# Score heads without a gate: one 128-row stationary [q hi; q lo] for both score matmuls

## The chip, the cores and the metric

The kernel runs on one core of one Trainium2 chip. The metric is the device time of one execution in microseconds; lower is better. TensorE (PE) does the matmuls, VectorE (DVE), ScalarE (ACT) and GpSimd (POOL) the elementwise work, and SyncE (SP) issues every DMA.

## The reference

Two transformer blocks run one after the other on 512 tokens of width 1024. The first has a pooling branch, twelve heads of dilated attention and a gated MLP. The second has four differential heads (two score maps each), six forgetting heads, six chunk heads, a convolution in its MLP and a final gated embedding. Every attention score has the same core, here from the second block:

```python
def probs(qb, k):
    s = jnp.einsum('bqhd,bkhd->bhqk', qb, k).astype(jnp.float32) * scale + bias
    s = jnp.where(allowed, s, NEG_INF)
    return jax.nn.softmax(s, axis=-1)
```

A head is 64 wide. The forgetting heads alone add a per-token gate (a cumulative sum of log f) to the score.

## The kernel before

All matmuls work on pairs of 32-bit tiles: a value x is kept as hi (x rounded to the matmul's type) and lo = x - hi, and a product is the sum of hi·hi, hi·lo and lo·hi. ACT makes hi and DVE makes lo (`split`, L179 and L180, or L182 and L183 with a scale).

The order of the attention stages is written out by hand in two strings, `ORDER1` (first block, `mix1`) and `ORDER2` (second block, `mix2`): P projects a pair of heads to q and k, T turns that pair into score operands, V makes values, S computes the four score blocks of one head, W transposes the probabilities and weighs the values. A planner then sets the order of instructions on each engine from this program, with its own estimate of durations; each engine executes its list in order.

T is `to_heads`. It transposes q and k of a pair (two heads of 64, L310) into two PSUM tiles, qT and kT, of 128 rows by 512 tokens. These come from a pool of three banks, from which projections and values take their banks too. It splits each of them over all 128 rows (two ACT and two DVE instructions), and then copies rows by DMA into operands: for each head, a tile k1 with k hi in the head's own 64 rows and k lo in the other 64, and a tile q1 with q hi in both halves. That is four copies of 64x512 a head, 128 KB each, eight a pair (`copy`, L379).

S calls `probs` for each block of 128 queries. Its two matmuls add into one bank: L255, of 128 stationary rows, gives hi·hi + hi·lo; L256 multiplies q lo by k hi. For heads without a gate L256 has the head's own 64 rows of the tiles, for the six forgetting heads 68 rows (64 plus four of the gate), copied to rows 0 to 67 of tiles of their own. The columns are 128, 256, 384 or 512. Then DVE adds the table (L259), ACT takes the exponential (L114), DVE the reciprocal (L263) and POOL scales (L267). W's transposes are L277, its matmuls L285 and L286. L189 to L191 and L352 to L354 are the three matmuls of a dense product.

There are 16 pairs, six in the first block and ten in the second. Three of them are the forgetting pairs; 13 have no gate.

Of the kernel before, what the change touches and what calls it, by code (L numbers as in the profile page):

```python
# [9 lines left out]
F32 = mybir.dt.float32  # L10
F32R = mybir.dt.float32r
AF = mybir.ActivationFunctionType
ALU = mybir.AluOpType
AX = mybir.AxisListType

P = 128
# [46 lines left out]
class Builder:  # L63
# [240 lines left out]
    def to_heads(self, z, gq, gk, extra=None):  # L304
        nc = self.nc
        qT, kT = self.psum(), self.psum()
        for d, o in ((qT, 0), (kT, P)):
            ins = {}
            for t in (3, 2, 1, 0):
                ins[t] = nc.tensor.transpose(d[:, t * P:t * P + P],  # L310
                                             z[t // 2][:, (t % 2) * 256 + o:(t % 2) * 256 + o + P], self.ident)
                if t < 3:
                    self.after(ins[t].ins, ins[3].ins.name)
        qh, ql = self.split(qT, gq, tag="k")
        ops = []
        kh, kl = self.split(kT, 1.0 if gk is None else gk, tag="k")
        ks = [self.slot("k", F32R) for _ in range(2)]
        for e in range(2):
            a, b = slice(64 * e, 64 * e + 64), slice(64 - 64 * e, P - 64 * e)
            k1, q1 = ks[e], self.slot("k", F32R)  # L320
            self.copy(k1[b], kl[a])
            self.copy(k1[a], kh[a])
            self.copy(q1[a], qh[a])
            self.copy(q1[b], qh[a])
            if extra is None:
                ops.append((q1, k1, ql[a], k1[a]))
                continue
            fr, i = extra
            q2, k2 = self.slot("k", F32R), self.slot("k", F32R)
            self.copy(q2[0:64], ql[a])  # L330
            self.copy(k2[0:64], k1[a])
            self.copy(q2[64:68], fr[i][4 * e:4 * e + 4])
            self.copy(k2[64:68], fr[i][32 + 4 * e:36 + 4 * e])
            ops.append((q1, k1, q2[0:68], k2[0:68]))
        return ops
# [673 lines left out]
```

## Time and profile before

| | us |
|---|---|
| median of three timed runs | 1374.2 (1372.47 to 1374.73) |
| span of the profiled execution, first to last instruction | 1373.6 |
| PE busy in it | 1345.1 (98%) |
| DVE busy | 842.4 (61%) |
| ACT busy | 657.9 (48%) |
| attention of the first block | about 45 to 192 |
| attention of the second block | about 690 to 912 |

The profiled execution's span is 0.6 us under the median; no other time is given for it. A matmul's recorded duration contains time in which its neighbours run too, so the pace of PE is read from the distance between the starts of successive matmuls, not from durations. The busy share says little about the attention stages, where the stretches with many small matmuls must be read one by one.

### The profile page before, as it was taken

The page shows a single profiled execution, that of the slowest core. Times are in us where ns is not written, and L with a number is a line of the kernel's source. Part 1 is how long each engine was busy: PE and PEld are TensorE (multiplying, and loading weights), DVE is VectorE, ACT ScalarE, POOL GpSimd, SP SyncE. Part 2 cuts the span into 40 slices and gives each one's busy share as a digit, 9 for nine tenths or more (in the row PEclk, how much of TensorE's full clock was granted, in tenths as well). Part 3 has the DMA queues.
Part 4 walks back from the last instruction along what each step waited for, and adds up shares of the span by engine and source line. Part 5 has one row for each costly group of instructions (what it writes and reads, how often), then busy time and mean ns, then how long its engine had stood idle before and what let it go on. Part 6 is the DMA issues. An engine that isn't in the chain of part 4 may idle for free.

```text
span 1373.6 us, 20168 instructions
## 1 busy us (share of the span) xinstructions
PE 1345.1 (98%) x7450; PEld 1147.6 (84%) x7450; DVE 842.4 (61%) x1713; ACT 657.9 (48%) x1285; POOL 206.6 (15%) x240
## 2 busy tenths in 40 slices
PE   9999999899999999997999999999999999999998
PEld 9888878788888888886988899778888888888887
DVE  6666785864444433239667877666777777743345
ACT  6465645543333332236465767664554444522242
POOL 1223222400000000016222334441000000000010
PEclk9999999999999999998999999999999999999999
DMA  5532433132233322326264345433432223332222
GB/s 199 142 95 67 117 103 123 50 120 92 92 95 103 95 92 92 95 84 229 93 155 125 104 121 147 110 100 115 140 99 92 92 92 98 101 101 92 92 92 77
DMA packets 52962, 148.52 MB, mean 108 GB/s; under 512 B 7072, under 2 KB 7968, under 8 KB 52864
## 3 DMA queue, kind: packets, MB, share of 16 engines
q1 hardware_dynamic: 52864, 147.24, 35.0%
q8 instruction: 58, 0.95, 0.3%
q14 instruction: 40, 0.33, 0.1%
HBM read 122.38 MB, written 6.29 MB: 94 GB/s over the span
## 4 chain that ended last, share of the span: by engine, by line
PE 89%; DVE 6%; DMA 2%; issue 1%; ACT 1%; POOL 1%; SPq 0%; DVEq 0%; POOLq 0%; ACTq 0%
PE p L190 20%; PE p L189 20%; PE p L191 20%; PE p L352 6%; PE p L353 6%; PE p L354 6%; PE p L256 3%; PE p L277 2%; PE p L255 2%; DVE sv L559 1%; PE p L286 1%; DVE sh L183 1%; PE p L285 1%; DVE wl L170 1%; PE p L310 1%
## 5 line engine op out<-in xcount | busy, mean ns | idle before, releaser
L166 ACT ACTIVATE wh<-wr 128x512 fp32r<-128x512 f32 x417 | 260.5, 631 | 409.9 <-PE p L190 350.4
L170 DVE TENSOR_TENSOR wl<-wr,wh 128x512 fp32r<-128x512 f32 x398 | 285.9, 724 | 224.7 <-ACT wh L166 218.2
L190 PE MATMUL p<-sh,wh 128*128 128x512 f32 (+1 forms) x858 | 323.1, 378 | 8.6 <-DVE sh L183 8.6
L191 PE MATMUL p<-sh,wl 128*128 128x512 f32 (+1 forms) x858 | 322.5, 377 | 0.0
L189 PE MATMUL p<-sh,wh 128*128 128x512 f32 (+1 forms) x858 | 318.6, 376 | 0.0
L352 PE MATMUL p<-wh,sh 128*128 128x256 f32 (+1 forms) x736 | 212.4, 290 | 3.3 <-ACT sz L446 2.4
L354 PE MATMUL p<-wh,sh 128*128 128x256 f32 (+1 forms) x736 | 210.7, 288 | 4.6 <-DVE sh L183 4.6
L353 PE MATMUL p<-wl,sh 128*128 128x256 f32 (+1 forms) x736 | 211.8, 289 | 0.2 <-DVE wl L170 0.2
L190 PEld LDWEIGHTS p<-sh,wh 128*128 128x128 f32 x858 | 162.7, 190 | 40.7 <-DVE sh L183 10.2
L191 PEld LDWEIGHTS p<-sh,wl 128*128 128x128 f32 x858 | 162.9, 190 | 31.5 <-issue 0.7
L189 PEld LDWEIGHTS p<-sh,wh 128*128 128x128 f32 x858 | 161.3, 190 | 32.0 <-issue 1.0
L352 PEld LDWEIGHTS p<-wh,sh 128*128 128x128 f32 x736 | 141.4, 192 | 8.3 <-issue 2.9
L354 PEld LDWEIGHTS p<-wh,sh 128*128 128x128 f32 x736 | 140.8, 192 | 8.0 <-DVE sh L183 5.7
L353 PEld LDWEIGHTS p<-wl,sh 128*128 128x128 f32 x736 | 141.3, 193 | 3.6 <-issue 1.9
L267 POOL TENSOR_SCALAR sp<-sp,m 128x128 f32<-128x128 f32 (+1 forms) x112 | 69.7, 626 | 181.4 <-DVE m L263 164.2
L114 ACT ACTIVATE sp<-sp,m 128x128 f32<-128x128 f32 (+3 forms) x128 | 71.6, 561 | 45.6 <-DVE m L259 42.1
L170 POOL TENSOR_TENSOR wl<-wr,wh 128x512 fp32r<-128x512 f32 (+1 forms) x19 | 25.6, 1345 | 447.9 <-ACT wh L166 447.7
L191 PE MATMUL p<-so,wl 128*128 128x512 f32 (+1 forms) x246 | 88.4, 360 | 0.2 <-DVE wl L170 0.2
L190 PE MATMUL p<-so,wh 128*128 128x512 f32 (+1 forms) x246 | 88.4, 360 | 0.0
L259 DVE CUSTOM_DVE_ANT_0 sp<-p,sm 128x128 f32<-128x128 f32 (+3 forms) x128 | 61.1, 486 | 44.3 <-PE p L256 32.4
L189 PE MATMUL p<-so,wh 128*128 128x512 f32 (+1 forms) x246 | 87.9, 361 | 0.2 <-ACT so L179 0.2
L190 PE MATMUL p<-sk,wh 128*128 128x512 f32 (+1 forms) x184 | 67.1, 365 | 0.0
(201 smaller groups left out, 2075.0 us busy)
## 6 DMA issues: line engine op xcount, KB each, us to landing
wr<-in_w_gu SPq DMA_DIRECT2D x88, 512.0 KB
wr<-in_w_down SPq DMA_DIRECT2D x44, 512.0 KB
sk<-sk SPq DMA_DIRECT2D x140, 128.0 KB
wr<-in_w_qk SPq DMA_DIRECT2D x31, 512.0 KB
wr<-in_w_out SPq DMA_DIRECT2D x12, 512.0 KB
sv<-in_x SPq DMA_DIRECT2D x16, 256.0 KB
wr<-in_w_ple_gate SPq DMA_DIRECT2D x8, 512.0 KB
wr<-in_w_v SPq DMA_DIRECT2D x6, 512.0 KB
```

Source lines behind the costliest of these rows:

```text
L114: i = self.nc.scalar.activation(out, in_, func, **k)
L166: nc.scalar.activation(hi[:, :w], c, AF.Copy)
L170: eng.tensor_tensor(lo[:, :w], c, hi[:, :w].bitcast(F32), ALU.subtract)
L189: mm(out, lhsT=ahi, rhs=bhi, start=start, stop=False)
L190: mm(out, lhsT=ahi, rhs=blo, start=False, stop=False)
L191: mm(out, lhsT=alo, rhs=bhi, start=False, stop=stop)
L256: nc.tensor.matmul(ps[:, :n], lhsT=q2[:, c], rhs=k2[:, :n], start=False, stop=True)
L259: nc.vector.tensor_tensor_reduce(p[:, :n], ps[:, :n], tab[:, (3 - qb) * P:S], 1.0, 3e38, ALU.add, ALU.min, accum_out=m[:, 0:1])
L267: self.nc.gpsimd.tensor_scalar(p[:, :n], p[:, :n], m[:, 2:3], 1.0, ALU.mult, ALU.mult)
L352: mm(d, lhsT=h[k][0][:, a], rhs=hi[:, c], start=k == 0 and (o == 0 or not first), stop=False)
L353: mm(d, lhsT=h[k][0][:, a], rhs=lo[:, c], start=False, stop=False)
L354: mm(d, lhsT=h[k][1][:, a], rhs=hi[:, c], start=False, stop=k == 7 and (o > 0 or not first))
```

## The change

For pairs without a gate `to_heads` now makes the operands by itself, head by head. With a the head's own 64 rows and b the other 64: ACT writes q hi to rows a of a tile q, and DVE writes q lo to rows b of the same tile, reading rows a. ACT writes k hi to rows a of a tile kh, DVE k lo to rows a of a tile kl. Two DMA copies then double kh and kl into rows b. Both score matmuls have q as their stationary operand, with 128 rows; the first has kh as its moving operand, the second kl. Together they give hi·hi + lo·hi + hi·lo + lo·lo. The forgetting pairs keep the old way, in a function of their own.

```diff
+        if extra is not None:
+            return self.heads_with_rows(qT, kT, gq, gk, *extra)
+        ops = []
+        gk = 1.0 if gk is None else gk
+        per = lambda g, r: g if isinstance(g, float) else g[r]
+        for e in range(2):
+            a, b = slice(64 * e, 64 * e + 64), slice(64 - 64 * e, P - 64 * e)
+            q, kh, kl = (self.slot("k", F32R) for _ in range(3))
+            nc.scalar.activation(q[a], qT[a], AF.Copy, scale=per(gq, a))
+            nc.vector.scalar_tensor_tensor(q[b], qT[a], per(gq, a), q[a].bitcast(F32), ALU.mult, ALU.subtract)
+            nc.scalar.activation(kh[a], kT[a], AF.Copy, scale=per(gk, a))
+            nc.vector.scalar_tensor_tensor(kl[a], kT[a], per(gk, a), kh[a].bitcast(F32), ALU.mult, ALU.subtract)
+            self.copy(kh[b], kh[a])
+            self.copy(kl[b], kl[a])
+            ops.append((q, kh, q, kl))
+        return ops
+
+    def heads_with_rows(self, qT, kT, gq, gk, fr, i):
         qh, ql = self.split(qT, gq, tag="k")
+        kh, kl = self.split(kT, gk, tag="k")
         ops = []
-        kh, kl = self.split(kT, 1.0 if gk is None else gk, tag="k")
...
-            if extra is None:
-                ops.append((q1, k1, ql[a], k1[a]))
-                continue
-            fr, i = extra
```

In the changed file the four new instructions are L322 and L324 (ACT), L323 and L325 (DVE); later lines are numbered 14 higher (the copy L393, projections L366 to L368). The tiles sk are score operands, p is PSUM, wh and wl are weights, sz a projected pair.

On ACT, at the first pair of the first block, before (a bracket names the engines waited for):

```order
L446 ACTIVATE sz_593<-p_544 128x512 [waits DVE_49,PE_49,Pool_49]
L182 ACTIVATE sk_611<-p_601 128x512 [waits PE_49]
L182 ACTIVATE sk_615<-p_602 128x512 [waits PE_49]
L166 ACTIVATE wh_1003<-wr_1001 128x512 [waits DMAHW0_49,Activation_49]
L374 ACTIVATE sv_631<-p_635,rc_204 128x4x64 [waits PE_49]
```

And now:

```order
L460 ACTIVATE sz_593<-p_544 128x512 [waits DVE_49,PE_49,Pool_49]
L322 ACTIVATE sk_611<-p_601 64x512 [waits PE_49]
L324 ACTIVATE sk_612<-p_602 64x512 [waits PE_49]
L322 ACTIVATE sk_620<-p_601 64x512 [waits DVE_49]
L324 ACTIVATE sk_621<-p_602 64x512 [waits DVE_49]
L166 ACTIVATE wh_999<-wr_997 128x512 [waits DMAHW0_49,Activation_49]
L388 ACTIVATE sv_629<-p_633,rc_204 128x4x64 [waits PE_49]
```

Two instructions became four, and those of the second head wait for DVE, which reads the same PSUM tile for the first head.

On DVE at the same place, before:

```order
L170 TENSOR_TENSOR wl_986<-wr_979,wh_985 128x512
L183 SCALAR_TENSOR_TENSOR sk_612<-p_601,sk_611 128x512
L183 SCALAR_TENSOR_TENSOR sk_616<-p_602,sk_615 128x512
L453 TENSOR_TENSOR sz_593<-sz_593,sm_212 128x512
L454 TENSOR_TENSOR sz_593<-sz_593,sz_594 128x8x32
```

And now:

```order
L170 TENSOR_TENSOR wl_982<-wr_975,wh_981 128x512
L323 SCALAR_TENSOR_TENSOR sk_611<-p_601,sk_611 64x512
L325 SCALAR_TENSOR_TENSOR sk_613<-p_602,sk_612 64x512
L467 TENSOR_TENSOR sz_593<-sz_593,sm_212 128x512
L323 SCALAR_TENSOR_TENSOR sk_620<-p_601,sk_620 64x512
L468 TENSOR_TENSOR sz_593<-sz_593,sz_594 128x8x32
L469 TENSOR_TENSOR sz_593<-sz_593,sz_594 128x8x32
L325 SCALAR_TENSOR_TENSOR sk_622<-p_602,sk_621 64x512
```

The second head's two instructions stand in between the rotation of the next pair (L467 to L469).

On PE, at the first scores of the second block (rows 3802 to 3808 of PE's list; a matmul reads its moving and then its stationary tile), before:

```order
L352 MATMUL p_7134<-wh_7077,sh_5750 128x256
L353 MATMUL p_7134<-wl_7078,sh_5750 128x256
L255 MATMUL p_6841<-sk_6827,sk_6829 128x128
L256 MATMUL p_6841<-sk_6827,sk_6820 128x128
L255 MATMUL p_6849<-sk_6797,sk_6799 128x128
L256 MATMUL p_6849<-sk_6797,sk_6790 128x128
L354 MATMUL p_7134<-wh_7077,sh_5751 128x256
```

And now (rows 3754 to 3760):

```order
L366 MATMUL p_7032<-wh_7061,sh_5738 128x256
L367 MATMUL p_7032<-wl_7062,sh_5738 128x256
L255 MATMUL p_6825<-sk_6806,sk_6805 128x128
L255 MATMUL p_6833<-sk_6778,sk_6777 128x128
L256 MATMUL p_6833<-sk_6779,sk_6777 128x128
L368 MATMUL p_7032<-wh_7061,sh_5739 128x256
L366 MATMUL p_7118<-wh_7035,sh_5724 128x256
```

The transposes of both pairs stand where they stood (from row 3697), so the first score has come 48 rows nearer to them; and the first matmul with k lo, L256 of the second pair, no longer follows its L255 at once.

## Rows read from the trace of the kernel before

**Rows 1.** The page: the chain that ended last, by engine.

```profile
PE 89%; DVE 6%; DMA 2%; issue 1%; ACT 1%; POOL 1%; SPq 0%; DVEq 0%; POOLq 0%; ACTq 0%
```

**Rows 2.** Timeline of PE: start us, duration us, line, tiles, rows*columns, moving operand; 64-row scores.

```profile
58.32 0.32 PE L256 MATMUL p<-sk,sk 64*128 64x128 f32 x1
58.58 0.38 PE L255 MATMUL p<-sk,sk 128*128 128x256 f32 x1
...
60.77 0.50 PE L255 MATMUL p<-sk,sk 128*128 128x512 f32 x1
61.20 0.50 PE L256 MATMUL p<-sk,sk 64*128 64x512 f32 x1
61.63 0.38 PE L352 MATMUL p<-wh,sh 128*128 128x256 f32 x1
...
69.29 0.40 PE L255 MATMUL p<-sk,sk 128*128 128x512 f32 x1
69.62 0.50 PE L256 MATMUL p<-sk,sk 64*128 64x512 f32 x1
...
908.37 0.50 PE L256 MATMUL p<-sk,sk 64*128 64x512 f32 x1
```

**Rows 3.** The same view at scores of forgetting heads, with 68 rows.

```profile
821.09 0.40 PE L255 MATMUL p<-sk,sk 128*128 128x512 f32 x1
821.33 0.40 PE L256 MATMUL p<-sk,sk 68*128 68x512 f32 x1
821.57 0.28 PE L352 MATMUL p<-wh,sh 128*128 128x256 f32 x1
...
825.22 0.28 PE L256 MATMUL p<-sk,sk 68*128 68x128 f32 x1
825.33 0.33 PE L353 MATMUL p<-wl,sh 128*128 128x256 f32 x1
```

**Rows 4.** Groups by form, count | busy us, mean ns | idle before: weight loads of L256.

```profile
L256 PEld LDWEIGHTS p<-sk,sk 64*128 64x128 f32 x104 | 19.3, 186 | 18.0 <-issue 13.1
L256 PEld LDWEIGHTS p<-sk,sk 68*128 68x128 f32 x24 | 4.5, 189 | 0.0
```

**Rows 5.** The same view: splits of T, and 64-row instructions of W.

```profile
L183 DVE SCALAR_TENSOR_TENSOR sk<-p,gq,sk 128x512 fp32r<-128x512 f32 x20 | 14.7, 742 | 1.6 <-ACT sk L182 1.4
L290 DVE TENSOR_TENSOR so<-p,st 64x512 f32<-64x512 f32 x28 | 19.2, 687 | 14.4 <-ACT st L289 13.9
L289 ACT ACTIVATE st<-p 64x512 f32<-64x512 f32 x28 | 16.6, 592 | 22.7 <-PE p L286 22.4
```

**Rows 6.** Timeline of SP's queue: the eight copies of one pair.

```profile
145.73 5.55 SPq L379 DMA_DIRECT2D sk<-sk  x8
```

**Rows 7.** Windows: stretch, length, busy us of PE, PEld, DVE, ACT, POOL, granted clock.

```profile
160.00:190.00 30.00, 30.00 (x147) 22.77 (x146) 26.27 (x74) 18.22 (x48) 10.30 (x13) 1.00 0.48 140
784.00:849.00 65.00, 65.00 (x525) 63.51 (x525) 48.60 (x146) 45.71 (x111) 27.29 (x31) 1.00 0.51 138
```

**Rows 8.** End of the first attention: timeline of DVE, then the chain (start, length, step).

```profile
178.13 0.68 DVE L290 TENSOR_TENSOR so<-p,st 64x512 f32<-64x512 f32 x1 [0.33 <-ACT st L289]
...
191.31 1.03 DVE wl L170
...
192.38 0.50 PE p L191
```

**Rows 9.** The chain in the second attention, 870 to 878 us.

```profile
870.44 0.60 PE p L277 x4
...
876.14 1.27 POOL sm L705
...
877.79 0.48 PE p L255
```

**Rows 10.** Timelines before the second block's first scores: DVE, then PE.

```profile
698.85 1.41 DVE L183 SCALAR_TENSOR_TENSOR sk<-p,gq,sk 128x512 fp32r<-128x512 f32 x2 [0.90 <-ACT sk L182]
...
706.29 0.22 PE L255 MATMUL p<-sk,sk 128*128 128x128 f32 x1
```

## The prediction

> **What bounds the kernel now.** I read the page's chain that ended last first: 89% of it is PE and 1% is issue [rows 1]. So time comes off this kernel only where PE's own list gets shorter, or where PE waits less. Next I read the timeline of PE around the scores, by the distance between successive starts. With 512 columns, a score of a forgetting head takes 0.24 us for L255 and 0.24 for L256 [rows 3]. The same block without a gate takes 0.43 and 0.43 at 60.77 us, or 0.33 and 0.43 at 69.29 [rows 2]. The columns are the same, the first matmul is the same; the difference is the second one, with 64 rows in place of 68. PE stands still on both sides of it: L256 starts 0.09 or 0.19 late, and what follows starts 0.19 late. The groups by form tell it too: the 104 weight loads of 64 rows have 18.0 us of idle time before them, 13.1 of it with no releaser that the profile shows, the 24 of 68 rows none [rows 4]. That it is no wait for data follows from the regularity, and from the missing releaser.
>
> **The gain: L256 with 128 rows.** The part after: for 384 and 256 columns I find the same 0.19 as for 512; for 128 columns it is 0.26 from start to start against 0.11 with 68 rows [rows 2, 3], 0.15 more. That makes 78 x 0.19 + 26 x 0.15 = 18.7 us. The part before, counted through the timeline from the first such matmul at 58.32 to the last at 908.37 [rows 2]: 54 times about 0.09 and 50 times about 0.19, 14.4 us. Together 33.1. Now and then a 68-row pair also loses up to 0.08, so I take 32. All of this lies on PE, so all of it is on the path where PE has nothing else to wait for. The changed L256 has the same 128 rows as L255, so I charge it 0.24 at 512 columns. The nearest row is the 68-row one [rows 3]; the bounds are no gain at all (if it were not the rows) and 33.
>
> That PE can run through score stretches without the pauses is shown by the forgetting stretch from 784 to 849 us: PE is busy all of it, DVE for 48.60 of 65 us, ACT for 45.71, and the clock is full [rows 7]. So the other engines can feed a PE that never pauses, at 75% of DVE.
>
> A rule of the Trainium skill speaks against this part: "TensorE: Matmul & The Clock Gate", section "LDWEIGHTS (loading the stationary operand)", says that a load's time goes by its columns and not by the rows, so that fewer rows cost no less and no more. The loads' durations agree (186 ns with 64 rows, 189 with 68 [rows 4]); by that alone the gain would be nothing. The start distances do not agree, and "TensorEngine Tiling (Array Packing)", section "Tiling Modes", has a rule that fits them: changing the tiling mode drains the engine. By it the 33 us go.
>
> **What the splits add.** For each of 13 pairs two ACT and two DVE instructions become four and four. Half the rows make none of them shorter: a 64x512 instruction of W takes 592 ns on ACT and 687 on DVE, the 128x512 split 742 on DVE [rows 5]. So 26 more on ACT, 26 x 0.59 = 15.3 us, and 26 more on DVE, 26 x 0.69 = 17.9 us, over two stretches of 147 and 222 us. DVE's write to rows other than it reads has no row; ACT's copy from one half to the other is L289 and takes the usual time, so I charge no more; the bounds are 17.9 us, all on the path, and nothing. I take nothing in general, because both engines have idle time beside a busy PE [rows 7], and charge the three places where cover is thin.
>
> *First, the end of the first attention: 2 us.* From 160 to 190 us DVE is busy 26.27 of 30 us [rows 7]. Its last idle moment is at 178.13; from there it runs solid, and the chain leaves PE for DVE until PE goes on at 192.38 [rows 8]. PE loses 12 L256 with their pauses in those 30 us, 12 x 0.35 = 4.2, and would be through in 25.8; DVE has two more instructions there, 26.3 + 1.4 = 27.7. So about 2 of the 4.2 cannot be had. Some DVE work can slip behind 190, or more of it come from before 160: bounds 0 and 4.
>
> *Second, the hole from 870 to 878: 1.5 us.* The chain leaves PE at 871.04 for ACT, DVE and POOL, and PE takes up again at 877.79 [rows 9]. Four of the L256 lie between, with pauses of about 0.37 us each. Their going shortens nothing, since the table of L705 and the softmax steps are late there anyway. Bounds 0 and 3.
>
> *Third, from T to S: 2 us.* The planner brings some first scores nearer to their transposes. In the first scores of the second block it is 48 rows of about 0.118 us, 5.7 us: 706.29 becomes about 700.6 [rows 10]. Before, the splits of the second pair ran on DVE from 698.85 to 700.26 [rows 10]. Now k lo of its first head is the second DVE instruction, ready at about 700.3 or a little later, and then its copy has to be issued and to land. A copy takes SP about 0.69 us to issue (5.55 for eight [rows 6]); no row has the landing, so I bound it by 0 and 3 us. So PE stands there for 0.4 to 4 us, less what the planner put between L255 and its L256. Two such approaches in the first block have some 5 us from the transposes to the score; they can lose up to 1 us each. I take 2 for all, bounds 0 and 6.
>
> **What hides, and its price.** SP issues four copies a pair and not eight, so 52 issues fewer, 36 us of SP's queue by the same row. SP is not on the path; the copies were off it too, since no score waited for them. Loads behind the copies go out earlier; nothing waits for those either. ACT's instructions for the second head now wait for DVE (the order of ACT shows the bracket), and behind them stand weight splits and exponentials. A pair holds qT and kT for two split steps more, some 1.3 us, of the three banks that the projections share. If PE has no bank then, it waits that long. I take it as covered, since the next projection mostly has a bank of its own in work by then; the bounds are 0 and 13 x 1.3 = 17 us.
>
> **Sum.** 1373.6 - 32 + 2 + 1.5 + 2 = 1347.1 us of span. The median stands 0.6 above the profiled span: 1347.7, so 1348.
>
> **Rivals.**
> *All of it arrives, and no place costs anything.* 1374 - 33 = 1341, give or take 2. For it speaks the forgetting stretch [rows 7]; against it the DVE chain at 192 [rows 8]. 0.15.
> *The banks are the new wait.* The two extra steps hold the banks and PE waits for most pairs: 1348 + 17 = 1365, from 1357 to 1371. For it: three banks, two of them held. Against it: the idle time of PE now is next to nothing, so there was room of unknown size. 0.15.
> *The rows are not the price.* If the pause came from q lo's own tile, or from any second weight load, the change would not do what it says: no gain, and the three places no dearer than now: 1374 to 1377. The 68-row pairs read a q lo tile of their own too, without a pause [rows 3], which is against it. 0.05. (The Trainium skill's rule on loads, in "TensorE: Matmul & The Clock Gate", would give this.)
> *Slower: ACT locked to DVE.* The second head's ACT instructions wait for DVE, DVE's list has score blocks in between that wait for PE, and the exponentials queue behind on ACT. If each pair stalls PE for 2 us beyond the forecast, 13 x 2 = 26 us, the gain is gone; at 3 us the time is 1348 + 39 = 1387. It decides from 2 us a pair on. Against it: DVE has the first head's split early in its list, ahead of score blocks. 0.05.
>
> **How the numbers follow.** The forecast, 1343 to 1357, has 0.60, and 1348 is its time. Two in ten may lie outside the range: below 1339 a few hundredths, above 1362 the upper half of the bank rival and the last two rivals. So 1339 to 1362. A measurement of this kernel tells about 0.2%, 2.7 us. Faster than that are the forecast, the full gain and the banks, 0.90; within it most of the fourth case, 0.04; slower the rest, 0.06.
>
> **What would show it.** L256 without a gate must start 0.24 us after its L255 at 512 columns, and the idle time before its weight loads must go to about zero; if 0.09 or 0.19 remains, the rows were not it. DVE's busy time should rise by about 18 us and ACT's by 15, with SP's copies down to 88. New waits of PE would show in the waits as PE for ACT or DVE on the bank of a projection (banks), or for sk (T to S). At the end of the first attention, DVE should stand on the chain longer than 187 to 192. I am wrong if PE waits for more than 10 us in the two attentions, or if the granted clock falls in a new stretch there.

## The result, and the profile after

The changed kernel takes 1362.0 us (median of four runs, 1361.7 to 1363.8); the kernel before takes 1373.3 beside it. The ratio is 0.9919 [0.9905, 0.9933]: 11.3 us faster, where 26 were forecast. The time stands at the upper end of the range, 1339 to 1362. The profiled execution's span is 1362.0.

The page after: first PE's busy time (share, instructions) and that of the others, then the chain by engine, which answers to [rows 1].

```profile
PE 1319.5 (97%) x7450; PEld 1146.2 (84%) x7450; DVE 862.6 (63%) x1739; ACT 674.2 (50%) x1311; POOL 205.5 (15%) x240
...
PE 83%; DVE 10%; DMA 2%; issue 2%; ACT 2%; POOL 0%; SPq 0%; DVEq 0%; ACTq 0%; POOLq 0%
```

PE's busy time fell by 25.6 us, but the span by only 11.6: PE now stands idle for 42.5 us in place of 28.5. Its share of the chain fell from 89 to 83%; DVE's rose from 6 to 10%.

The pauses are gone. PE's timeline after, scores without a gate (columns as in [rows 2]):

```profile
60.53 0.42 PE L255 MATMUL p<-sk,sk 128*128 128x384 f32 x1
60.79 0.34 PE L256 MATMUL p<-sk,sk 128*128 128x384 f32 x1
60.97 0.40 PE L255 MATMUL p<-sk,sk 128*128 128x512 f32 x1
61.20 0.40 PE L256 MATMUL p<-sk,sk 128*128 128x512 f32 x1
62.55 0.30 PE L255 MATMUL p<-sk,sk 128*128 128x128 f32 x1 [0.96 <-ACT sp L114]
```

At 512 columns L256 starts 0.23 us after its L255; before it was 0.33 or 0.43 [rows 2]. The last line shows the new thing: the next score starts only at 62.55, after PE has stood idle for 0.96 us, by the profile until an exponential (L114) was done. The groups of weight loads answer to [rows 4] and say the same; first L255 before, then L255 and L256 after:

```profile
L255 PEld LDWEIGHTS p<-sk,sk 128*128 128x128 f32 x128 | 24.5, 191 | 5.4 <-issue 1.6 <-DVE m L259 1.4 <-DVE m L659 0.3
...
L255 PEld LDWEIGHTS p<-sk,sk 128*128 128x128 f32 x128 | 24.2, 191 | 9.7 <-DVE m L259 7.2 <-ACT sp L114 1.4 <-DVE sz L505 0.7
L256 PEld LDWEIGHTS p<-sk,sk 128*128 128x128 f32 x104 | 19.9, 192 | 0.8 <-DMA sk<-sk 0.6
```

The 18.0 us before L256 are 0.8. Before L255 there are now 9.7 us of idle time in place of 5.4, 7.2 of them with DVE's L259 as releaser, which had 1.4.

The work that was added has the size that was worked out: DVE is 20.2 us busier (forecast 18), ACT 16.3 (forecast 15), and SP issues 88 copies for 140. The instructions on the operand tiles after, for the copies and DVE's two new splits, answer to [rows 5, 6]: count, then shortest, median and longest ns, first and last start.

```profile
L393 SPq DMA_DIRECT2D sk<-sk x88: 461/510/1401, 48.3 to 880.3; - x88
...
L323 DVE SCALAR_TENSOR_TENSOR sk<-p,gq,sk x14: 743/750/756, 684.9 to 877.2; 64x512 fp32r<-64x512 f32 x14
L325 DVE SCALAR_TENSOR_TENSOR sk<-p,gq,sk x14: 720/749/758, 686.3 to 879.5; 64x512 fp32r<-64x512 f32 x14
```

L323 writes to other rows than it reads, L325 to the same rows: 750 and 749 ns, so the crossing costs DVE nothing that these rows show. Half the rows save nothing: the 128-row split took 742 ns [rows 5].

Windows over the two attentions, before and then after: stretch, length, busy us of PE, PEld, DVE, ACT and POOL, granted clock. Of after also the two stretches of [rows 7].

```profile
40.00:210.00 170.00, 167.33 (x1077) 143.62 (x1077) 120.07 (x312) 95.35 (x222) 45.13 (x64) 0.99 0.37 105
660.00:930.00 270.00, 268.25 (x1860) 238.05 (x1860) 193.47 (x589) 172.09 (x419) 92.66 (x107) 0.99 0.44 123
```

```profile
40.00:210.00 170.00, 162.76 (x1121) 149.73 (x1120) 130.93 (x327) 104.58 (x237) 46.86 (x66) 0.98 0.31 92
660.00:930.00 270.00, 259.21 (x1853) 239.10 (x1852) 203.25 (x592) 179.86 (x427) 87.85 (x105) 0.98 0.38 110
160.00:190.00 30.00, 28.25 (x142) 23.03 (x143) 29.72 (x75) 19.69 (x46) 10.29 (x10) 1.00 0.31 91
784.00:849.00 65.00, 63.89 (x495) 61.50 (x494) 50.83 (x148) 49.82 (x116) 22.83 (x29) 0.97 0.45 127
```

PE's idle time in the two attentions went from 2.7 + 1.8 us to 7.2 + 10.8. The prediction called itself wrong if PE waited for more than 10 us there, or if the granted clock fell in a new stretch. Both came: it is 0.97 from 784 to 849 us, where it had been 1.00.

### The profile page after: what moved, and what is told of

It is laid out like the page before. It is cut to its first block, busy times and chain, and to the rows that moved or that the text cites. A ratio compares the mean times of both kernels' runs of the same rounds, so it can differ in the third digit from the quotient of the medians.

```text
span 1362.0 us, 20144 instructions
## 1 busy us (share of the span) xinstructions
PE 1319.5 (97%) x7450; PEld 1146.2 (84%) x7450; DVE 862.6 (63%) x1739; ACT 674.2 (50%) x1311; POOL 205.5 (15%) x240
## 4 chain that ended last, share of the span: by engine, by line
PE 83%; DVE 10%; DMA 2%; issue 2%; ACT 2%; POOL 0%; SPq 0%; DVEq 0%; ACTq 0%; POOLq 0%
PE p L190 21%; PE p L189 21%; PE p L191 20%; PE p L368 5%; PE p L367 5%; PE p L366 5%; PE p L277 2%; DVE wl L170 1%; DVE sp L259 1%; DVE sv L573 1%; DVE sh L183 1%; PE p L286 1%; PE p L285 1%; PE p L255 1%; PE p L256 1%
## 5 line engine op out<-in xcount | busy, mean ns | idle before, releaser
L170 DVE TENSOR_TENSOR wl<-wr,wh 128x512 fp32r<-128x512 f32 x398 | 287.7, 728 | 224.0 <-ACT wh L166 217.8
L366 PE MATMUL p<-wh,sh 128*128 128x256 f32 (+1 forms) x736 | 211.2, 289 | 4.3 <-ACT sz L460 2.2
L368 PE MATMUL p<-wh,sh 128*128 128x256 f32 (+1 forms) x736 | 210.2, 288 | 5.2 <-DVE sh L183 5.2
L368 PEld LDWEIGHTS p<-wh,sh 128*128 128x128 f32 x736 | 141.4, 193 | 7.3 <-DVE sh L183 6.4
L366 PEld LDWEIGHTS p<-wh,sh 128*128 128x128 f32 x736 | 141.9, 193 | 6.3 <-ACT sz L460 2.5
L170 POOL TENSOR_TENSOR wl<-wr,wh 128x512 fp32r<-128x512 f32 (+1 forms) x19 | 25.3, 1329 | 450.6 <-ACT wh L166 441.7
L114 ACT ACTIVATE sp<-sp,m 128x128 f32<-128x128 f32 (+3 forms) x128 | 71.5, 559 | 40.8 <-DVE m L259 37.6
L259 DVE CUSTOM_DVE_ANT_0 sp<-p,sm 128x128 f32<-128x128 f32 (+3 forms) x128 | 60.2, 483 | 19.5 <-PE p L256 9.6
```

The costliest lines, as they stand in the source:

```text
L114: i = self.nc.scalar.activation(out, in_, func, **k)
L170: eng.tensor_tensor(lo[:, :w], c, hi[:, :w].bitcast(F32), ALU.subtract)
L259: nc.vector.tensor_tensor_reduce(p[:, :n], ps[:, :n], tab[:, (3 - qb) * P:S], 1.0, 3e38, ALU.add, ALU.min, accum_out=m[:, 0:1])
L366: mm(d, lhsT=h[k][0][:, a], rhs=hi[:, c], start=k == 0 and (o == 0 or not first), stop=False)
L368: mm(d, lhsT=h[k][1][:, a], rhs=hi[:, c], start=False, stop=k == 7 and (o > 0 or not first))
```

## The experiments

Times are medians; ratios are against the kernel before on the same chip, with their 95% intervals. For comparisons between experiments a ratio is turned into us by 1374. The accounting at the end of this section uses the profiled executions.

### The old splits, with 128 rows in L256

The kernel before, with one line changed: L256 reads the whole tiles. Every engine's list stays in its order. The 64 rows that come in add the other head's q lo by the head's own k lo. That product does not belong to the score; as lo by lo it is of rounding size.

```diff
-                ops.append((q1, k1, ql[a], k1[a]))
+                ops.append((q1, k1, ql, k1))
```

> The kernel before with one edit: the second matmul of a score without a gate takes the full 128-row tiles ql and k1, so its product is not the score's (it adds rows of the other head). Splits, copies and the order of every engine are those of before; the pauses around 64 rows alone are gone. Theory A (what the splits add took the rest of the gain): PE keeps nearly all, 1341 to 1347. Rival B (the pauses covered waits for DVE that the old splits have too): 1356 to 1364, with new waits of PE for DVE in both attentions.

Measured: 1343.1 us, 0.9778 [0.9762, 0.9794]. That is 31.1 us for the pauses alone. It is the fastest version but one, 19 us ahead of the changed kernel by the medians. Below it is called the one-line kernel. Its weight loads of L256:

```profile
L256 PEld LDWEIGHTS p<-sk,sk 128*128 128x128 f32 x104 | 19.7, 189 | 0.3
```

The same tiles, the same second weight load, the same order: only the rows differ, and the pauses go. So the rows were the price.

### The changed kernel, with 64 rows in L256

The second matmul reads only the rows of q lo and of k lo in the other half, so the score lacks q hi by k lo. Again every engine's list stays in its order.

```diff
-            ops.append((q, kh, q, kl))
+            ops.append((q, kh, q[b], kl[b]))
```

> The changed kernel with one edit: the second matmul takes the other half's 64 rows, q lo by k lo, so the score lacks q hi by k lo. Splits, copies and the order of every engine are those of the changed kernel; the pauses are back. Theory A: the pauses cover most of what the splits add, 1374 to 1380. Rival C (the new splits and the new order cost PE time whatever it does): 1384 to 1394, the changed time plus 24 to 32. Rival B: 1372 to 1376.

Measured: 1383.3 us, 1.0066 [1.0045, 1.0088]. The idle time before L256 is back:

```profile
L256 PEld LDWEIGHTS p<-sk,sk 64*128 64x128 f32 x104 | 18.9, 183 | 17.4 <-issue 12.5
```

So the new splits, copies and order cost 9.2 us (6 to 12 by the interval) in a kernel that pauses. In one that doesn't they cost 18.9 us, by the medians 1362.0 and 1343.1. The time lies between the two ranges expected: about half of the price was hidden behind the pauses, not most of it and not none. This is the main result: the gain of the pauses and the price of the splits can't simply be added.

### The load by itself

The one-line kernel, with two ACT and two DVE instructions of 64x512 per pair that write to a tile that nobody reads.

```diff
+        if extra is None:
+            scr = self.slot("k")
+            for hi, lo in ((qh, ql), (kh, kl)):
+                nc.scalar.activation(scr[0:64], hi[0:64].bitcast(F32), AF.Copy)
+                nc.vector.tensor_tensor(scr[64:128], hi[64:128].bitcast(F32), lo[64:128].bitcast(F32), ALU.subtract)
```

> The version without pauses and with the old splits (e1), and beside each split of a pair without a gate two more ACT and two more DVE instructions of 64x512 that read the split tiles and write a scratch tile nobody reads: the changed kernel's load on both engines, without a longer chain to the scores and without a bank held longer. If load takes the gain: 1354 to 1362. If waiting between ACT and DVE inside a split, or the banks, take it: 1343 to 1349.

Measured: 1350.2 us, 0.9827 [0.9803, 0.9851]: 6.7 us above the one-line kernel, between the two ranges expected. DVE is 17.7 us busier than in the one-line kernel and ACT 11.4; in the changed kernel it is 22.3 and 17.3. But the planner gives new lists as soon as anything is added, so the next two runs ask what that alone costs.

### Another order, the same work

The one-line kernel with k split before q, and the one-line kernel with the copies of q issued before those of k.

```diff
-        qh, ql = self.split(qT, gq, tag="k")
         ops = []
         kh, kl = self.split(kT, 1.0 if gk is None else gk, tag="k")
+        qh, ql = self.split(qT, gq, tag="k")
```

> The same base (e1), with k's split written ahead of q's: nothing added or removed, but the planner puts other orders together. It says how much the order of the engines' lists is worth by itself. If the order is worth little: 1341 to 1346. If a good part of the changed kernel's loss is that its lists are others than the ones the hand-written order was made with: 1348 to 1360.

```diff
-            self.copy(k1[b], kl[a])
-            self.copy(k1[a], kh[a])
             self.copy(q1[a], qh[a])
             self.copy(q1[b], qh[a])
+            self.copy(k1[a], kh[a])
+            self.copy(k1[b], kl[a])
```

> A second neutral reordering of the version without pauses (e1): the copies of q written ahead of those of k, nothing added or removed. If a new order alone is worth about 6, as in the first reordering: 1346 to 1352. If the first was a bad draw: 1341 to 1345.

Measured: 1349.0 us, 0.9817 [0.9796, 0.9839], and 1348.0 us, 0.9796 [0.9777, 0.9814]: 5.4 and 2.5 us above the one-line kernel. The first's interval lies just clear of the one-line kernel's, the second's overlaps it. The load's 6.7 us can't be told from the first of these. Less the one or the other, 1 to 4 us are left for the load; each of these intervals is 2 to 3 us to either side, so that its price may also be nothing.

### ACT and DVE in turn on one bank

The one-line kernel, with each split made in two halves of the columns. In the first kernel ACT and DVE take turns on a bank; ACT's second half waits for DVE's first. In the second, ACT writes both halves of hi and then DVE both halves of lo. The instructions are the same in both.

```diff
...
+            for c in (slice(0, 256), slice(256, S)):
+                self.split(qT, gq, qh, ql, cols=c)
+                self.split(kT, gk, kh, kl, cols=c)
...
```

> The same base (e1), each split made in two column halves, ACT and DVE in turn on the same PSUM tile: the changed kernel's four steps on a bank and ACT's wait for DVE, but with instructions of 256 columns (about 0.40 us each and not 0.6 to 0.7), so only some 5 us more on each engine in all and not 15 to 18. If the lock or the banks take the gain: 1354 to 1362. If load takes it: 1344 to 1349.

```diff
...
+            cs = (slice(0, 256), slice(256, S))
+            for hi, g, d in ((qh, gq, qT), (kh, gk, kT)):
+                for c in cs:
+                    nc.scalar.activation(hi[:, c], d[:, c], AF.Copy, scale=g)
+            for hi, lo, g, d in ((qh, ql, gq, qT), (kh, kl, gk, kT)):
+                for c in cs:
+                    nc.vector.scalar_tensor_tensor(
+                        lo[:, c], d[:, c], g, hi[:, c].bitcast(F32), ALU.mult, ALU.subtract)
...
```

> The control of the run with column halves (e8): the same instructions of 256 columns, but ACT's two for a bank first and then DVE's two, so that ACT never waits for DVE inside a split. Same load, and another new order. If the lock costs: 1347 to 1352, about 6 under that run. If a new order costs some 6 to 13 by chance, and the lock nothing: 1353 to 1358.

Measured: 1356.4 us, 0.9871 [0.9852, 0.989], and 1349.9 us, 0.9814 [0.98, 0.9829]. The intervals are apart: taking turns, with the order that the planner then makes, costs 7.8 us. Without it the cut splits are 4.9 us above the one-line kernel, no more than another order is.

### The changed kernel without the turns, and without the held banks

First: all four ACT instructions of a pair ahead of its four DVE instructions. Second: ACT copies qT and kT whole to SBUF (26 more instructions of 128x512), and the splits read those, so that a bank is free after one instruction.

```diff
...
+        for (a, b), (q, kh, kl) in zip(half, ts):
             nc.scalar.activation(q[a], qT[a], AF.Copy, scale=per(gq, a))
+        for (a, b), (q, kh, kl) in zip(half, ts):
+            nc.scalar.activation(kh[a], kT[a], AF.Copy, scale=per(gk, a))
+        for (a, b), (q, kh, kl) in zip(half, ts):
             nc.vector.scalar_tensor_tensor(q[b], qT[a], per(gq, a), q[a].bitcast(F32), ALU.mult, ALU.subtract)
-            nc.scalar.activation(kh[a], kT[a], AF.Copy, scale=per(gk, a))
...
```

> The changed kernel with the split of a pair written in another order: ACT's four instructions first, then DVE's four, so that no ACT instruction of a pair waits for DVE. The planner moves other work a little. If ACT waiting for DVE within a pair is what costs: 1350 to 1356. If DVE's load or its list costs: 1359 to 1365.

```diff
+        raws = []
+        for d in (qT, kT):
+            raw = self.slot("k")
+            nc.scalar.activation(raw, d, AF.Copy)
+            raws.append(raw)
+        qT, kT = raws
```

> The changed kernel, with qT and kT first copied whole from PSUM to SBUF by ACT (26 instructions of 128x512 more on ACT, some 16 us), and the splits made from those copies. A bank is then held for one ACT step instead of four steps, and no ACT instruction waits for DVE on a bank; DVE's load is the changed kernel's. If the banks and the lock make up most of the 19 us between the version without pauses and the changed kernel: 1348 to 1354. If DVE's and ACT's load does: 1358 to 1366, more load giving more.

Measured: 1357.1 us, 0.9875 [0.9856, 0.9893], and 1352.5 us, 0.9843 [0.9826, 0.9859], against 0.9919 [0.9905, 0.9933] for the changed kernel. The first lies between the two ranges expected, the second in the range for the banks and the turns. The second gives ACT 26 more instructions (15.0 us; ACT's busy time rises by 9.2) and is 10 us faster than the changed kernel. That suggests that the amount of work on ACT and DVE matters less than whom they wait for and how long they keep a bank. It is not shown, since the planner's order changed here too. The changed kernel's timeline at the second block's first transposes shows banks that are kept, PE first, then DVE, then ACT:

```profile
689.13 0.63 PE L310 MATMUL p<-ident,sz 128*128 128x128 f32 x4 [1.77 <-DVE sk L323]
690.63 0.35 PE L366 MATMUL p<-wh,sh 128*128 128x256 f32 x1 [0.87 <-DVE sk L325]
...
688.23 0.76 DVE L323 SCALAR_TENSOR_TENSOR sk<-p,gq,sk 64x512 fp32r<-64x512 f32 x1 [1.16 <-ACT sk L322]
...
689.73 0.76 DVE L325 SCALAR_TENSOR_TENSOR sk<-p,gq,sk 64x512 fp32r<-64x512 f32 x1
691.10 0.74 DVE L323 SCALAR_TENSOR_TENSOR sk<-p,gq,sk 64x512 fp32r<-64x512 f32 x1 [0.62 <-ACT sk L322]
...
686.86 0.63 ACT L166 ACTIVATE wh<-wr 128x512 fp32r<-128x512 f32 x1 [0.95 <-DMA wr<-in_w_qk]
687.51 0.68 ACT L322 ACTIVATE sk<-p,gq 64x512 fp32r<-64x512 f32 x1
```

Read upwards from the last line: ACT stood behind a weight split that waited for its transfer, DVE waited for ACT's q hi, and PE had no bank until DVE had made the second head's q lo and then its k lo, the last readings of qT and kT (688.23 + 0.76, then 689.73 + 0.76). ACT did not wait for DVE here; what kept the banks was the chain of steps behind a late weight. With the copies to SBUF the profile lists no wait of PE from 680 to 692 us, and in neither attention one that a split of q or k ends.

### Fewer extra instructions, more copies

First: only q is made by halves, k by the old splits and eight copies. Second: both by the old splits, with twelve copies a pair.

```diff
+        kh, kl = self.split(kT, gk, tag="k")
...
-            nc.scalar.activation(kh[a], kT[a], AF.Copy, scale=per(gk, a))
-            nc.vector.scalar_tensor_tensor(kl[a], kT[a], per(gk, a), kh[a].bitcast(F32), ALU.mult, ALU.subtract)
-            self.copy(kh[b], kh[a])
-            self.copy(kl[b], kl[a])
+            self.copy(k1[a], kh[a])
+            self.copy(k1[b], kh[a])
+            self.copy(k2[a], kl[a])
+            self.copy(k2[b], kl[a])
...
```

> Half of the changed kernel's splits: q by head halves on the engines (four instructions a pair), k by the two old 128-row instructions and eight copies. 13 more instructions on ACT and on DVE than before, and not 26; as many copies as before. If the loss goes with the number of added instructions or steps, it lies halfway between 1343 and 1362: 1350 to 1356. If any new order of the lists costs some 10: 1352 to 1358 too, with waits elsewhere.

```diff
+        qh, ql = self.split(qT, gq, tag="k")
+        kh, kl = self.split(kT, gk, tag="k")
...
+            self.copy(q[a], qh[a])
+            self.copy(q[b], ql[a])
+            self.copy(k1[a], kh[a])
+            self.copy(k1[b], kh[a])
+            self.copy(k2[a], kl[a])
+            self.copy(k2[b], kl[a])
...
```

> The changed kernel's operands made the old way: two ACT and two DVE instructions of 128 rows a pair, and twelve copies (52 more than before in all, 104 more than changed). Correct scores, no pauses, 26 instructions fewer on ACT and on DVE than changed. Theory A: 1342 to 1350, less if the copies come late. Rival B: 1356 to 1364. If the copies of a pair on SP's queue (twelve by 0.69 us) come too late for the scores: 1360 and more, with PE waiting for copies of sk.

Measured: 1353.2 us, 0.9843 [0.9816, 0.9871], and 1354.9 us, 0.9859 [0.9839, 0.9879]. Half the extra instructions, about half the price; but both of the ranges expected hold that time, so it does not tell load from order. Twelve copies have no extra instruction on ACT or DVE and still stand 11 us above the one-line kernel, in none of the ranges expected. PE waits for `sk` to land at three places there, 0.47, 0.50 and 0.99 us; the rest is not told apart from the new order. The changed kernel, with its splits and four copies, is another 7 us slower than this. What four copies are worth against eight no run shows.

### A faster version?

The one-line kernel, with every fourth weight lo of the first attention on POOL.

```diff
+        self.share = SHARE
         self.play(ORDER1, P=project, T=heads, V=values, S=score, W=weigh, U=pool_in,
                   B=lambda: self.pool_branch(us, oT))
+        self.share = 0
```

> The version without pauses (e1), with every fourth weight split of the first attention on POOL and not on DVE, as the second attention has it: nine instructions of 0.7 us less on DVE there, nine of 1.3 more on POOL, in a stretch where PE still waits 0.7 us for DVE. If DVE's load at the end of the first attention holds PE: 1340 to 1342. If not, or if POOL comes late with weights: 1343 to 1348.

Measured: 1342.9 us, 0.9762 [0.9746, 0.9779], the same as the one-line kernel within the intervals. It did not make DVE lighter: with nine instructions fewer DVE is busy for 840.6 us, against 840.3. One of the instructions on POOL, and DVE's beside it:

```profile
110.40 1.67 POOL L170 TENSOR_TENSOR wl<-wr,wh 128x512 fp32r<-128x512 f32 x1 [1.58 <-ACT wh L166]
111.06 1.56 DVE L170 TENSOR_TENSOR wl<-wr,wh 128x512 fp32r<-128x512 f32 x1
```

In the one-line kernel DVE's L170 of 128x512 takes 688 ns in the mean, and 695 at most, where no instruction of POOL runs beside it (344 of them), and 989 in the mean where one does (50). So this run does not tell what a lighter DVE would be worth.

### Where the time stands in each

The clock has two levels, 2.4 GHz (1.00) and 1.2 (0.50). So (1 - mean clock) x span is the time that work at the lower level lost, if PE was busy all through it. PE's busy time less that is what PE's list would take at full clock:

| profiled execution | span | PE busy | idle | clock | lost to clock | list at full clock |
|---|---|---|---|---|---|---|
| before | 1373.6 | 1345.1 | 28.5 | 0.987 | 17.9 | 1327.2 |
| changed, 64 rows | 1381.6 | 1348.1 | 33.5 | 0.987 | 18.0 | 1330.1 |
| changed | 1362.0 | 1319.5 | 42.5 | 0.985 | 20.4 | 1299.1 |
| changed, ACT first | 1355.5 | 1314.0 | 41.5 | 0.989 | 14.9 | 1299.1 |
| changed, copies to SBUF | 1352.8 | 1312.6 | 40.2 | 0.990 | 13.5 | 1299.1 |
| one line, in turn | 1354.2 | 1316.2 | 38.0 | 0.988 | 16.3 | 1299.9 |
| one line, not in turn | 1347.8 | 1311.9 | 35.9 | 0.991 | 12.1 | 1299.8 |
| one line, load | 1348.2 | 1313.6 | 34.6 | 0.989 | 14.8 | 1298.8 |
| one line, k first | 1347.3 | 1312.3 | 35.0 | 0.989 | 14.8 | 1297.5 |
| one line, copies of q first | 1346.5 | 1311.1 | 35.4 | 0.990 | 13.5 | 1297.6 |
| one line | 1341.4 | 1309.0 | 32.4 | 0.991 | 12.1 | 1296.9 |
| one line, lo on POOL | 1338.5 | 1308.6 | 29.9 | 0.991 | 12.0 | 1296.6 |
| only q by halves | 1346.5 | 1310.9 | 35.6 | 0.990 | 13.5 | 1297.4 |
| twelve copies | 1353.2 | 1315.9 | 37.3 | 0.987 | 17.6 | 1298.3 |

The clock is read to 0.001, which is 1.4 us of a span, so the last two columns are good to about 0.7 us. The last column is 1297 to 1300 wherever L256 has 128 rows, and 1327 to 1330 where it has 64. All else is idle time and clock. From the one-line kernel to the changed one, 20.6 us of span are 10.1 idle, 8.3 clock and 2.2 of list. (The clock's part rests on one execution of each; over all runs, the changed kernel's clock is 0.985 to 0.987 and the one-line kernel's 0.989 to 0.991, which makes it nearer to 5.) The kernel before shows how much of the clock is one execution's: the profiled one stands at 0.987, most others at 0.989 to 0.992. Span and mean clock, first of the changed kernel and then of the one-line kernel:

```profile
core 0: 1362.0 us, clock 0.985
```

```profile
core 0: 1341.4 us, clock 0.991
```

What PE did before the clock fell is seen best at 98 to 112 us, in windows of the changed kernel:

```profile
98.00:101.00 3.00, 3.00 (x27) 2.88 (x25) 3.00 (x9) 2.98 (x8) 0.00 (x0) 1.00 0.58 172
101.00:103.00 2.00, 1.38 (x9) 1.15 (x7) 1.94 (x5) 1.98 (x8) 0.09 (x1) 1.00 0.77 205
103.00:105.00 2.00, 1.25 (x6) 0.85 (x6) 2.00 (x7) 1.93 (x6) 0.28 (x1) 0.95 0.35 127
105.00:108.40 3.40, 2.94 (x14) 2.91 (x15) 3.24 (x13) 2.57 (x7) 1.11 (x3) 0.53 0.34 77
108.40:112.00 3.60, 3.60 (x30) 3.51 (x29) 2.32 (x8) 2.04 (x6) 1.94 (x3) 1.00 0.17 39
```

and at about the same place in the one-line kernel, then in the kernel before:

```profile
96.00:102.00 6.00, 6.00 (x50) 5.91 (x49) 5.29 (x18) 5.22 (x13) 1.67 (x4) 1.00 0.33 100
102.00:108.00 6.00, 6.00 (x48) 5.78 (x47) 3.24 (x12) 3.41 (x11) 2.85 (x6) 1.00 0.66 154
...
98.00:105.00 7.00, 7.00 (x46) 5.68 (x45) 5.88 (x17) 5.75 (x14) 0.98 (x2) 1.00 0.48 153
```

DVE and ACT are both all but full from 98 to 105 us in the changed kernel (6.94 and 6.89 of 7 us); before they were at 5.88 and 5.75, with the pauses still in PE. PE runs out of work, is busy for 2.63 of 4 us, and then the clock stands at 1.2 GHz for 3.4 us. The Trainium skill, "TensorE: Matmul & The Clock Gate", section "A second HAM failure mode: psum-queue depth-cycling", says that many short idle spells of PE between groups of matmuls are enough to bring its clock down now and then. The trace fits that in size, not in number: no single wait in that stretch is over 0.76 us, but only two of them, 0.76 and 0.62 us, come before the fall.

A wait does not always bring the clock down. At the start of the first attention PE waits equally long for ACT in the kernel before and in the one-line kernel; each wait is followed here by the window from 44 to 48 us, first before, then the one-line kernel:

```profile
45.20 0.58 PE L352 MATMUL p<-wh,sh 128*128 128x256 f32 x1 [2.42 <-ACT sz L446]
44.00:48.00 4.00, 2.80 (x13) 2.80 (x14) 4.00 (x8) 1.58 (x3) 2.14 (x2) 0.65 0.38 134
...
45.67 0.38 PE L352 MATMUL p<-wh,sh 128*128 128x256 f32 x1 [2.42 <-ACT sz L446]
44.00:48.00 4.00, 2.33 (x19) 2.33 (x20) 3.97 (x8) 1.58 (x3) 2.16 (x2) 1.00 0.36 106
```

The clock is 0.65 in the one and 1.00 in the other. The changed kernel has that wait too (2.22 us), with a fall behind it: from 40 to 60 us its clock is 0.91, as in the kernel before. So a part of the 8.3 us stands where the splits added nothing.

Why DVE is late at 104 us in the changed kernel is read from its timeline, with PE's score at the end:

```profile
101.86 0.68 DVE L323 SCALAR_TENSOR_TENSOR sk<-p,sk 64x512 fp32r<-64x512 f32 x1
102.58 0.16 DVE L263 RECIPROCAL m<-m 128x1 f32<-128x1 f32 x1
102.66 0.54 DVE L259 CUSTOM_DVE_ANT_0 sp<-p,sm 128x384 f32<-128x384 f32 x1
103.12 0.08 DVE L259 DVE_READ_ACCUMULATOR2_ANT m<- 128x1 f32 x1
103.12 0.68 DVE L325 SCALAR_TENSOR_TENSOR sk<-p,sk 64x512 fp32r<-64x512 f32 x1
103.73 0.67 DVE L259 CUSTOM_DVE_ANT_0 sp<-p,sm 128x512 f32<-128x512 f32 x1
...
104.46 0.38 PE L255 MATMUL p<-sk,sk 128*128 128x256 f32 x1 [0.62 <-DVE m L259]
```

The new splits stand between the score steps. L325 at 103.12 delays L259 by 0.61 us, and the next score, which needs a bank that L259 must have read, waits 0.62. The longer wait, 0.76 us at 103.13, ends with ACT's L179 and not with DVE.

## Why the prediction was half right

*The gain, 32 us: right.* The one-line kernel measures it alone as 31.1 by the medians; the column of the list gives 30.3 (1327.2 to 1296.9) and 31.0 (1330.1 to 1299.1). The rival that the rows are not the price is out, by the same runs. The rule that changing the tiling mode drains the engine fits (the Trainium skill, "TensorEngine Tiling (Array Packing)", section "Tiling Modes"): 17.4 us of idle time before the loads with 64 rows in the changed kernel, 0.8 with 128. That a drain is what the pauses are, no run shows by itself.

*What the splits add: the step that failed.* The prediction took their 15 + 18 us as nothing in general and charged three places, 5.5 us. With the copies and the order that came along they cost some 19 in a kernel without the pauses. What failed in it has two parts. First, the cover was read from a mean: DVE at 75% over 65 us [rows 7]. From 98 to 105 us it is at 99%, with ACT at 98%, and one such bunch is enough for PE to wait. Second, those 65 us hold only scores of forgetting heads, which neither pause nor have new splits. The pairs that were changed stood where PE paused, and there the pauses were themselves cover: the same splits with 64 rows cost 9.2 us. Taking away 31 us of PE time uses up the slack of the others in the same step.

*The clock: no term of the sum.* The prediction named its fall as what would make it wrong, and gave it no price. Of the 19 us, 8.3 are clock by the table, and some 5 over all runs. It moves the other comparisons too: from the kernel before to the one-line kernel the span falls by 32.2 us, of which 30.3 are list and 5.8 clock, against 3.9 more idle time. Those 5.8 are luck of the profiled executions: over all runs beside each other the two kernels' clocks do not differ (0.989 to 0.992 and 0.989 to 0.991).

*The banks, taken as covered, bounds 0 to 17.* By name they cost 2.6 us (1.77 and 0.87, at 689 and 691 us). But with the copies to SBUF the changed kernel is 10.4 us faster, and 9.2 by the profiled spans: 2.3 idle, 6.9 clock. The rival "the banks are the new wait" has the measured time in its 1357 to 1371, but by luck, since the wait is mostly not where it put it: "PE waits for most pairs" is wrong, two new waits are all.

*ACT locked to DVE.* The rival had the mechanism and not its size: it needed 2 us a pair to undo the gain. Taking turns costs 7.8 us over 13 pairs in the one-line kernel, 0.6 a pair; in the changed kernel, ACT first saves 6.0 by the ratios. In both comparisons the planner's order differs too, and the few us that another order costs lie within these numbers.

*End of the first attention, 2 us: near in size, not in its reason.* PE's idle time from 160 to 190 us went from 0 to 1.75 [rows 7], and DVE is busy 29.72 of 30. But only 0.77 us of it stand where the chain goes through DVE:

```profile
180.18 0.50 PE L189 MATMUL p<-so,wh 128*128 128x512 f32 x1 [0.50 <-DVE m L259]
185.20 0.50 PE L191 MATMUL p<-so,wl 128*128 128x512 f32 x1 [0.27 <-DVE wl L170]
```

The one-line kernel, without the new splits, has 0.95 there (0.74 and 0.21). Nor does DVE stand on the chain longer: it stands there from 179.57 to 185.16, 5.6 us, and before from 186.74 to 192.34.

*From T to S, 2 us: too high.* The first score of the second block starts at 696.25 with no idle time before it [rows 10]; PE's only wait for a copy of `sk` is 0.4 us in all. *The hole, 1.5 us:* it is still there, but its size can't be set against the 1.5, since PE has other waits around it now, and the clock is at 1.2 GHz behind it. Two steps of the changed kernel's chain (start, length, step), and the wait of PE that follows, from the timeline:

```profile
861.29 5.16 DMA sm<-in_tab_rel
...
866.60 1.27 POOL sm L719
```

```profile
868.24 0.44 PE L255 MATMUL p<-sk,sk 128*128 128x384 f32 x1 [1.66 <-DVE m L259]
```

POOL's table step stood at 876.14 before [rows 9] and stands at 866.60, 9.5 us earlier, behind a transfer of 5.16 us; PE waits 1.66 us for DVE's step after it.

*What stays open.* How the 10 us of idle time share out between load, turns and banks. Each run that removes one of them also gets another order from the planner, and another order alone is worth 2.5 to 5.4 us. That the clock falls behind waits was seen at 105 us and again at 845 (PE busy 1.89 of 3 us, then 0.57 for 3.5 us); that the waits are the cause was not tried by itself, and at 45 us the same wait came with a fall and without one.

## What to carry to other kernels

Before a matmul operand is remade to get rid of a short row count, see whether the tiles that exist already have 128 rows: one line that reads whole tiles, whose extra rows multiply to rounding size or to nothing, took the whole 31 us here, and the kernel with remade operands gave 19 of it back. Slack beside an engine that pauses is no slack once the pauses go, so work that is added in the same change must be charged against the stretches where two engines are full at once, not against a mean over a stage. Where two engines read one PSUM tile, let each do all its reads in one go, or copy the tile out first; here the one was worth 7.8 and the other 10.4 us, each with the planner's new order in it.

## What the runs showed of the hardware

- A matmul of 64 stationary rows among those of 128 costs about 0.3 us beyond its own time (31.1 us / 104), one of 68 rows costs nothing of the kind [rows 3].
- A DVE split of 64x512 that writes to the other 64 rows takes 750 ns, one that writes to the same rows 749, and one of 128x512 742: half the rows are no cheaper, and the crossing is free.
- Where an instruction of POOL runs beside it, DVE is slower: its weight split L170 of 128x512 takes 989 ns in the mean, against 688 alone (one-line kernel; POOL's spans are rough).
- After some waits of PE of under 1 us close together its clock stood at 1.2 GHz for 3.4 us. After one wait of 2.42 us it fell in one kernel and not in another. Between the one-line and the changed kernel the clock weighs half as much as the waits themselves, or more: 10.1 us idle, 5 to 8.3 clock. The runs of the kernel before show the same: 1371.7 us at a mean clock of 0.992, 1377.3 at 0.987.
